# A diffusion block on one Trainium2 core: the queries' inverse norm moved into the attention's exponential, and the context's row pieces spaced ten weights apart

## The chip, the cores and the metric

The kernel runs on one NeuronCore of one Trainium2 chip. The metric is the device time of one launch in microseconds (us). Three runs of the kernel before took 1333.79, 1327.81 and 1338.1 us; their median is 1333.79. A fourth execution was profiled. It took 1332.48 us, and its profile spans 1330.7 us from the first to the last instruction, so 1.8 us lie outside the span.

## The reference, cut to what matters

One layer over 512 latent tokens with 256 context tokens beside them. Both are normalised and modulated, then projected; the context gives only keys and values. Queries and keys get an RMS norm per head (128 channels), the latents' also a rotation; the softmax runs over 768 keys.

```python
q = _rope(_rmsnorm(_heads(p, OFF_Q, N_Q_HEADS), q_norm_g[l]), cos, sin) * q_scale
k = _rope(_rmsnorm(_heads(p, OFF_K, N_KV_HEADS), k_norm_g[l]), cos, sin)
kc = _rmsnorm(_heads(pc_kv, 0, N_KV_HEADS), k_norm_g[l])       # context
s = jnp.einsum('bqhgd,bkhd->bhgqk', qi, k, preferred_element_type=jnp.float32)
w = jax.nn.softmax(s, axis=-1).astype(v.dtype)
```

The inverse norm is one positive number per token and head. A product of a query row with it multiplies that row's 768 scores by the same number, so it may be applied to the query or to the scores.

## The kernel before, in words

**Products in three matmuls.** Every fp32 operand is split into a high part and a low rest. ScalarE (ACT) writes the high part (line 163), VectorE (DVE) subtracts it from the source and writes the rest (line 164), and each product is then three matmuls (lines 305 to 307): high with high, with the low part of the weights (306), and low data with high weights. A weight piece is 128x1024. Three of every five go to `whi` and `wlo`; the other two go as two halves of 128x512 to tiles called `s`.

**The weights' queue.** `stream` lists every piece in order of use. `start_load` issues its DMA (line 202, or 205 for the first piece of a chain) on the SP queue as soon as one of some six raw buffers is free; `get` splits the pieces ahead of the one that the matmuls take (`split_piece`). Some pieces are sums: a chain tile `R` (four of them, one per piece `pc` 0 to 3) gets `R += wr` on DVE (line 250), or an accumulating DMA from GpSimd's queue (line 261), which is issued once the split that reads `R` is done. For the product P7 DVE forms `wr = R - wr` (line 252), which needs both the load of `wr` and the accumulating DMA into `R`.

**The groups.** The input projection runs in eight groups, `KINDS = (qz, qz, qz, gate, gate, kv, gate, gate)`. Each has seven products of four weight pieces, in the order P1, Q5, P2, Q6, P7, Q3, Q4: a scheme with seven half-size products in the place of eight. A piece keeps TensorE busy for about 2.7 us (12 matmuls). A `qz` group gives 512 channels of queries and 512 of a gate; when a half of the queries is ready, `qz_done` calls `rotated`.

**`rotated`** (lines 838 to 858) takes 256 tokens by 4 heads. ACT squares and sums per token and head into `ss`, 8 columns of `sums`; DVE multiplies by the cosines (849) and the sines (851); GpSimd turns the sums into inverse roots (`root_of`); DVE adds the two products (854), multiplies the sum by the inverse norm (855, a 128x1024 product), and transposes 32x32 blocks (857). The result goes to DRAM (`q_d`). `kv_done` calls the same function for the keys.

**The context's rows.** The context's normalised and modulated rows are made in four parts, while the two gate groups 3 and 4 run. `context_piece` says after which weight piece each is made: counted from group 3's first piece, after the pieces 18, 24, 30 and 36 of the two groups' 56. `context_row(i, raw)` makes one: four DVE multiplications (line 976), one subtraction (979), six more with shifts (985), ACT's additions of the shifts (988, 989), then a store of 896 KB to DRAM (990, `cf_d`). All four use the one tile `qr`, so a part's first multiplication waits until the part before has been stored. Its 512 KB of raw rows take one of the weights' raw buffers. `context_norm` and `context_spread`, which make the factor of the tokens, run from a list of jobs, one job per piece. The kv group (5) reads `cf_d` back, and puts its rotation tables into `qr` (lines 821 and 822).

**Attention.** For each of 12 heads and 4 blocks of 128 queries, `scores(i)` makes 128x768 scores in PSUM; DVE takes the negated row maximum (line 1130), ACT the exponential with this as bias and its row sum (1132). `turn(i)` transposes the probabilities on TensorE (1148) and splits them, `divide(i)` puts the inverse sum into the gate's rows (1141, 1142), `values` multiplies with the values. Branch B's products (`fill`) lie between.

**What sets the order.** The code above fixes what depends on what. The framework's scheduler then lists each engine's instructions by its own estimates of durations, and each engine runs its list in order. So an edit can move instructions that it does not name.

Of the kernel before, what the change touches and what calls it, by code (L numbers as in the profile page):

```python
# [12 lines left out]
ACT = mybir.ActivationFunctionType  # L13
ALU = mybir.AluOpType
# [4 lines left out]
P = 128  # L19
# [4 lines left out]
HD = 128  # L24
# [3 lines left out]
NKEY = T + C  # L28
# [36 lines left out]
def context_piece(g, name, pc):  # L65

    n = 28 * (g - NQZ) + 4 * ONE_GROUP.index(name) + pc
    if n % 2 == 0 and 0 <= n < 8:
        return "cn", n // 2
    if n % 6 == 0 and 18 <= n < 42:  # L70
        return "cr", n // 6 - 3

# [33 lines left out]
def block_kernel(ctx, tc, xT, ctx_rows, ctx_toks, x, c_row, w_ss, w_gate, vecs, qkg, rope, dft_c, dft_s,  # L108
                 w_start, w_g, w_pab, w_o, final_g, out):
    nc = tc.nc  # L110
# [28 lines left out]
    def uid(s):  # L139
        cnt[0] += 1  # L140
        return f"{s}{cnt[0]}"
# [148 lines left out]
    def slot_tile(p, shape, dt):  # L290
        return p[0].tile([P] + list(shape), dt, tag=p[1], bufs=1, name=uid("s"))

    def take(shape, dt=F32, pool=None):
        p = next((p for p in free if p[0] is pool), free[0])
        free.remove(p)
        t = slot_tile(p, shape, dt)
        home[id(t)] = p, t
        return t

    def give(*ts):  # L300
        free.extend(home.pop(id(t))[0] for t in ts)

    def mm3(o, ah, al, bh, bl, start, stop, cont=False):

        nc.tensor.matmul(o, ah, bh, start=start, stop=False, skip_group_check=cont)  # L305
        nc.tensor.matmul(o, ah, bl, start=False, stop=False, skip_group_check=cont)  # L306
        nc.tensor.matmul(o, al, bh, start=False, stop=stop, skip_group_check=cont)  # L307
# [11 lines left out]
    small = const.tile([P, 6 * KK], F32, name="small")  # L319
# [57 lines left out]
    for g in range(LAST + 1):  # L377
        for name in ONE_GROUP:
            if (g, name) == (LAST, "Q4"):
                stream_keys(0)  # L380
            if g == KV:
                f = CTX_FORMS.index(next(f for n, f, _, _ in PRODUCTS if n == name))
                stream(("cf", name), cf_d[:, :, f].rearrange("i p j c -> p i j c"), 1024, 8, dst=ctx_tiles)
            stream_product(name, g, w_g[g], BY_DVE_GATES)
            for pc in range(4):
                p = context_piece(g, name, pc)
                if p:
                    src, cols = (ctx_toks[p[1]], 1024) if p[0] == "cn" else (ctx_rows[p[1]], 4 * C)
                    stream(p, src, cols, 1, "raw")
                    todo.insert(len(todo) - 4 + pc, todo.pop())  # L390
# [12 lines left out]
    for name in OUT_GROUP:  # L403
        stream_product(name, 8, w_o[1], BY_DVE_OUT)
        if name in DONE:
            half, c = DONE[name]
# [292 lines left out]
    def pair(tag, skip=0):  # L699
        if tag == "y":  # L700
            last_y[0] += 1 + skip
            return psp.tile([P, 2, 512], F32, tag=f"y{last_y[0] % 2}", bufs=1, name=uid(tag))
        return psp.tile([P, 2, 512], F32, tag=tag, bufs=2, name=uid(tag))
# [21 lines left out]
    class Group:  # L725
# [12 lines left out]
        def run(self, name):  # L738
# [10 lines left out]
            for pc in range(4):  # L749
                w = get((name, self.g, pc))  # L750
                for k in range(2):
                    for t in range(2):
                        self.mm(a, form, 2 * pc + k, t, w, start and pc == 0 and k == 0,
                                pc == 3 and k == 1, cont=not start)
                if self.more:
                    self.more.products(name, which, pc, w, start)
                for f, h, ready in between(self.g, name, pc):
                    if ready:
                        self.forms[f][4 * h : 4 * h + 4] = split_form(whole[f, h])
                    else:  # L760
                        make_form(f, h)
                job()
                p = None if self.last else context_piece(self.g, name, pc)
                if p:
                    (context_squares if p[0] == "cn" else context_row)(p[1], get(p))
# [65 lines left out]
    sums, stats = small[:, :32], gain.rearrange("p k j -> p (k j)")  # L831

    def root_of(ss, n=HD):

        nc.gpsimd.tensor_scalar(ss, ss, 1.0 / n, EPS, op0=ALU.mult, op1=ALU.add)
        nc.gpsimd.tensor_tensor(ss, ss, mhalf[:, : ss.shape[-1]], op=ALU.pow)

    def rotated(half, v, t2):

        v = v.rearrange("p t (h d) -> p t h d", h=4)  # L840
        r, t2 = new_q(), t2.rearrange("p t (h d) -> p t h d", h=4)
        ss = sums[:, 8 * half : 8 * half + 8]
        r5 = lambda w: w.rearrange("p h (a f j) -> p h a f j", a=2, f=2)
        for b in range(2):
            cosb, sinb = (turning[:, i, 2 * half + b, None, :].broadcast_to([P, 4, HD]) for i in range(2))
            for h in range(4):
                nc.scalar.activation(t2[:, b, h, :], v[:, b, h, :], ACT.Square,
                                     accum_out=ss[:, 4 * b + h : 4 * b + h + 1])
            nc.vector.tensor_tensor(r[:, b], v[:, b], cosb, op=ALU.mult)
            for f in range(2):  # L850
                nc.vector.tensor_tensor(r5(t2[:, b])[:, :, :, f, :], r5(v[:, b])[:, :, :, 1 - f, :],
                                        r5(sinb)[:, :, :, f, :], op=ALU.mult)
        root_of(ss)
        nc.vector.tensor_tensor(t2, r, t2, op=ALU.add)
        nc.vector.tensor_tensor(t2, t2, ss.rearrange("p (t h) -> p t h", t=2)[:, :, :, None].broadcast_to([P, 2, 4, HD]),
                                op=ALU.mult)
        nc.vector.transpose(r.rearrange("p t h d -> p (t h d)"), t2.rearrange("p t h d -> p (t h d)"))
        return r

    def qz_done(half, c, v, t):  # L860

        if c:
            e = pair("x" if half else "y")
            nc.scalar.activation(e, v, ACT.Tanh, scale=0.5)
            nc.vector.scalar_tensor_tensor(v, e, 1.0, v, op0=ALU.add, op1=ALU.mult)
            r = v.rearrange("p t (h d) -> p t h d", h=4)
        else:
            r = rotated(half, v, pair("y"))
        for b in range(2):
            t = 2 * half + b  # L870
            if c:
                nc.scalar.dma_start(z_d[4 * group.g : 4 * group.g + 4, :, t, :].rearrange("h p d -> p h d"), r[:, b])
            else:
                nc.scalar.dma_start(q_d[group.g, t].rearrange("p (h d) -> p h d", h=4), r[:, b])
# [3 lines left out]
    def kv_done(half, c, v, t):  # L878


        r = v.rearrange("p t (g d) -> p t g d", g=4) if c else rotated(half, v, pair("y", 1) if half else pair("x"))
        for b in range(2):
            if c:
                nc.scalar.dma_start(by_group(v_d[:, :, 2 * half + b, :]), r[:, b])
            else:
                nc.scalar.dma_start(k_d[2 * half + b].rearrange("p (h d) -> p h d", h=4), r[:, b])
# [147 lines left out]
    for g, kind in enumerate(KINDS):  # L1034
# [6 lines left out]
        elif g == KV + 1:  # L1041
            qzs.close()
            gvs, gvp = region("gvp", "right", reuse_waits="tile")
            hl_pools += range(MORE_HL)
        group = Group(g, forms, new_ev, {"qz": qz_done, "kv": kv_done, "gate": gate_done}[kind], {"a": "x", "b": "y", "c": "x"})
        if g == KV:
            group.more = Context()
# [70 lines left out]
    probs, pts, branch = {}, {}, {}  # L1118
    NSTEP = 4 * NH

    def scores(i):
        h, t = divmod(i, 4)
        kh, kl = kv[h // GQ][:2]
        s = slice(t * P, (t + 1) * P)
        qh, ql = qs[h][:, 0, s], qs[h][:, 1, s]
        sc = flat(pair("x"))
        for a, b in ((0, 512), (512, 768)):
            mm3(sc[:, a:b], qh, ql, kh[:, a:b], kl[:, a:b], True, True)
        mx = stats[:, 4 * (i % 4) : 4 * (i % 4) + 4]
        nc.vector.tensor_reduce(mx[:, 0:1], sc[:, :NKEY], axis=AX.X, op=ALU.max, negate=True)  # L1130
        probs[i] = take((NKEY,))
        nc.scalar.activation(probs[i], sc[:, :NKEY], ACT.Exp, bias=mx[:, 0:1], accum_out=mx[:, 1:2])  # L1132
        if t == 3:
            give(qs.pop(h))

# [56 lines left out]
    for i in range(NSTEP + 3):  # L1192
        h, t = divmod(i, 4)
        if i < NSTEP:
            if t == 1 and h + 2 < NH:
                load_head(h + 2)
            if i == 24:
                load_row(0)
            elif i == 28:
                silu_of_row(0)  # L1200
            if i % 12 == 10 and i // 12 + 1 < NKV:
                get_keys(i // 12 + 1)
            scores(i)
# [80 lines left out]
    for n, j in enumerate(CHUNKS):  # L1284
# [9 lines left out]
        for pc, t in products(j, accs) if n else first:  # L1294
# [4 lines left out]
            if pc > 3:  # L1299
                y = ybs[j, pc - 4]  # L1300
# [277 lines left out]
```

## Time and profile before

| what | value |
|---|---|
| runs of the kernel before | 1333.79, 1327.81, 1338.1 us |
| profiled execution: time, span | 1332.48 us, 1330.7 us |
| TensorE (PE) matmuls | 1293.6 us, 97% of the span, 6522 instructions |
| weight loads into TensorE (PEld) | 1055.5 us, 79% |
| VectorE (DVE) | 987.1 us, 74% |
| ScalarE (ACT) | 654.4 us, 49% |
| GpSimd (POOL) | 136.5 us, 10% |
| mean granted TensorE clock | 0.994 of full speed |
| DMA | 291.28 MB, mean 219 GB/s |

The page gives busy time by engine. As the matmuls are pipelined and overlap, 97% says that TensorE hardly ever stands still; the views that matter are the waits (who waited for whom, in total, how often, the longest) and the timeline of a stretch, where a row is an instruction with its start, its length, and in brackets the idle time of its engine before it and what ended that. Names of tiles stand as `out<-in`, without their numbers.

### The profile page before, as it was taken

The page shows a single profiled execution, that of the slowest core. Times are in us where ns is not written, and L with a number is a line of the kernel's source. Part 1 is how long each engine was busy: PE and PEld are TensorE (multiplying, and loading weights), DVE is VectorE, ACT ScalarE, POOL GpSimd, SP SyncE. Part 2 cuts the span into 40 slices and gives each one's busy share as a digit, 9 for nine tenths or more (in the row PEclk, how much of TensorE's full clock was granted, in tenths as well). Part 3 has the DMA queues.
Part 4 walks back from the last instruction along what each step waited for, and adds up shares of the span by engine and source line. Part 5 has one row for each costly group of instructions (what it writes and reads, how often), then busy time and mean ns, then how long its engine had stood idle before and what let it go on. Part 6 is the DMA issues. An engine that isn't in the chain of part 4 may idle for free. (4 is left out here: it accounts for less than half of the span.)

```text
span 1330.7 us, 17467 instructions
## 1 busy us (share of the span) xinstructions
PE 1293.6 (97%) x6522; PEld 1055.5 (79%) x6522; DVE 987.1 (74%) x1299; ACT 654.4 (49%) x1018; POOL 136.5 (10%) x186
## 2 busy tenths in 40 slices
PE   7999999999999999999998999999999999999996
PEld 3566887888888887888887888888888888878884
DVE  4655889888778878648485667778676789787677
ACT  5322655555555454444253555667565233464534
POOL 1110011110211111011021020000000100110210
PEclk9999999999999999999998999999999999999999
DMA  9996677877888899877659798442113988778973
GB/s 383 398 380 251 221 193 201 217 216 228 196 301 212 278 279 247 274 165 180 202 145 279 236 202 235 119 95 69 44 48 119 342 337 310 190 157 242 229 209 127
DMA packets 125718, 291.28 MB, mean 219 GB/s; under 512 B 46784, under 2 KB 60608, under 8 KB 121280
## 3 DMA queue, kind: packets, MB, share of 16 engines
q1 hardware_dynamic: 88912, 176.10, 40.0%
q0 software_dynamic: 21168, 91.24, 28.4%
q10 hardware_dynamic: 15552, 22.81, 4.9%
q8 instruction: 51, 0.84, 0.3%
q14 instruction: 35, 0.29, 0.1%
HBM read 263.37 MB, written 26.75 MB: 218 GB/s over the span
## 5 line engine op out<-in xcount | busy, mean ns | idle before, releaser
L163 ACT ACTIVATE whi<-wr 128x1024 fp32r<-128x1024 f32 (+1 forms) x129 | 135.4, 1052 | 188.5 <-PE y L307 77.4
L306 PE MATMUL y<-wlo,s 128*128 128x512 f32 x544 | 213.7, 393 | 5.3 <-DVE wlo L164 5.3
L306 PE MATMUL x<-wlo,s 128*128 128x512 f32 x548 | 214.4, 391 | 3.6 <-DVE wlo L164 3.6
L305 PE MATMUL y<-whi,s 128*128 128x512 f32 x544 | 214.9, 395 | 1.1 <-ACT s L772 1.1
L305 PE MATMUL x<-whi,s 128*128 128x512 f32 x548 | 214.5, 391 | 0.7 <-ACT whi L163 0.4
L307 PE MATMUL x<-whi,s 128*128 128x512 f32 x548 | 213.9, 390 | 0.0
L307 PE MATMUL y<-whi,s 128*128 128x512 f32 x544 | 213.3, 392 | 0.0
L164 DVE TENSOR_TENSOR wlo<-wr,whi 128x1024 fp32r<-128x1024 f32 (+1 forms) x129 | 155.4, 1210 | 54.1 <-ACT whi L163 53.6
L163 ACT ACTIVATE whi<-R 128x1024 fp32r<-128x1024 f32 x115 | 121.3, 1059 | 130.3 <-PE y L307 58.5
L164 DVE TENSOR_TENSOR wlo<-R,whi 128x1024 fp32r<-128x1024 f32 x115 | 139.7, 1219 | 50.3 <-ACT whi L163 50.1
L306 PEld LDWEIGHTS x<-wlo,s 128*128 128x128 f32 x548 | 103.3, 188 | 25.6 <-DVE wlo L164 4.5
L306 PEld LDWEIGHTS y<-wlo,s 128*128 128x128 f32 x544 | 102.8, 189 | 25.3 <-DVE wlo L164 6.2
L305 PEld LDWEIGHTS y<-whi,s 128*128 128x128 f32 x544 | 102.6, 189 | 23.6 <-ACT s L772 1.5
L305 PEld LDWEIGHTS x<-whi,s 128*128 128x128 f32 x548 | 103.3, 188 | 22.7 <-ACT whi L163 0.8
L307 PEld LDWEIGHTS x<-whi,s 128*128 128x128 f32 x548 | 103.3, 188 | 21.7
L307 PEld LDWEIGHTS y<-whi,s 128*128 128x128 f32 x544 | 102.7, 189 | 21.6
L306 PE MATMUL x<-s,s 128*128 128x512 f32 (+1 forms) x284 | 106.7, 376 | 0.0
L307 PE MATMUL x<-s,s 128*128 128x512 f32 (+1 forms) x284 | 105.7, 372 | 0.0
L305 PE MATMUL x<-s,s 128*128 128x512 f32 (+1 forms) x274 | 103.9, 379 | 1.0 <-ACT s L1132 0.9
L261 POOL DMA_DIRECT2D R<-in_w_g x64 | 55.1, 866 | 440.5 <-DVE wlo L164 314.9
L163 ACT ACTIVATE s<-wr 128x512 fp32r<-128x512 f32 (+2 forms) x98 | 65.2, 681 | 64.7 <-PE y L307 25.9
L164 DVE TENSOR_TENSOR s<-wr,s 128x512 fp32r<-128x512 f32 (+2 forms) x98 | 71.4, 750 | 27.6 <-ACT s L163 26.7
(273 smaller groups left out, 2240.7 us busy)
## 6 DMA issues: line engine op xcount, KB each, us to landing
wr<-in_w_g SPq DMA_DIRECT2D x128, 512.0 KB, 4.7
R<-in_w_g POOLq DMA_DIRECT2D x64, 512.0 KB, 7.0
wa<-in_w_ss POOLq DMA_DIRECT2D x28, 1024.0 KB, 8.7
R<-in_w_g SPq DMA_DIRECT2D x32, 512.0 KB, 5.0
wr<-in_w_pab SPq DMA_DIRECT2D x32, 512.0 KB, 5.0
wr<-in_w_gate SPq DMA_DIRECT2D x32, 512.0 KB, 5.5
wr<-in_w_o SPq DMA_DIRECT2D x24, 512.0 KB, 5.3
R<-in_w_o POOLq DMA_DIRECT2D x24, 512.0 KB, 7.1
```

The source lines that it names most:

```text
L163: nc.scalar.activation(hi, src, ACT.Copy)
L164: return nc.vector.tensor_tensor(lo, src, hi.bitcast(F32), op=ALU.subtract)
L261: nc.gpsimd.dma_start(chain[e.pc], e.nxt, accum_op=ALU.add)
L305: nc.tensor.matmul(o, ah, bh, start=start, stop=False, skip_group_check=cont)
L306: nc.tensor.matmul(o, ah, bl, start=False, stop=False, skip_group_check=cont)
L307: nc.tensor.matmul(o, al, bh, start=False, stop=stop, skip_group_check=cont)
```

## The change

Two edits.

1. `context_piece` puts the context's four row parts at the pieces 14, 24, 34 and 44, ten apart, in the place of 18, 24, 30 and 36.
2. The queries are no longer multiplied by their inverse norm in `rotated`. The inverse norms stay in SBUF, 16 columns for each of the three qz groups (`qss`, in columns of `small` that nothing reads any more at that time), so the queries' sums no longer share the columns of `sums`. In `scores` a DVE product of 128x1 multiplies the negated maximum by them, and the exponential takes them as its factor (`scale=r`). The keys are treated as before.

```diff
-    if n % 6 == 0 and 18 <= n < 42:
-        return "cr", n // 6 - 3
+    if n % 10 == 4 and 14 <= n < 54:
+        return "cr", n // 10 - 1
...
+    qss = [small[:, 32:48], small[:, 48:64], small[:, 80:96]]
+
+    def rotated(half, v, t2, ss, scaled):
...
-        ss = sums[:, 8 * half : 8 * half + 8]
...
         root_of(ss)
         nc.vector.tensor_tensor(t2, r, t2, op=ALU.add)
-        nc.vector.tensor_tensor(t2, t2, ss.rearrange("p (t h) -> p t h", t=2)[:, :, :, None].broadcast_to([P, 2, 4, HD]),
-                                op=ALU.mult)
+        if scaled:
+            nc.vector.tensor_tensor(t2, t2, ss.rearrange("p (t h) -> p t h", t=2)[:, :, :, None].broadcast_to([P, 2, 4, HD]),
+                                    op=ALU.mult)
...
-            r = rotated(half, v, pair("y"))
+            r = rotated(half, v, pair("y"), qss[group.g][:, 8 * half : 8 * half + 8], False)
...
         mx = stats[:, 4 * (i % 4) : 4 * (i % 4) + 4]
+        r = qss[h // 4][:, 4 * t + h % 4 : 4 * t + h % 4 + 1]
         nc.vector.tensor_reduce(mx[:, 0:1], sc[:, :NKEY], axis=AX.X, op=ALU.max, negate=True)
+        nc.vector.tensor_tensor(mx[:, 0:1], mx[:, 0:1], r, op=ALU.mult)
         probs[i] = take((NKEY,))
-        nc.scalar.activation(probs[i], sc[:, :NKEY], ACT.Exp, bias=mx[:, 0:1], accum_out=mx[:, 1:2])
+        nc.scalar.activation(probs[i], sc[:, :NKEY], ACT.Exp, bias=mx[:, 0:1], scale=r, accum_out=mx[:, 1:2])
```

The scheduler's lists move with it, in three places that matter below. In the lists the line numbers of the changed kernel are larger by 3 to 5 from `rotated` on.

**VectorE in group 0, where the first half of the queries is rotated.** `y` is the rotated half, `ev` and `S` are other forms and results of the group. Before:

```order
L854 TENSOR_TENSOR y_1836<-qr,y_1836 128x1024
L686 TENSOR_TENSOR ev_1940<-s_926,S_68 128x512
L855 TENSOR_TENSOR y_1836<-y_1836,small 128x1024
L687 TENSOR_TENSOR ev_1940<-ev_1940,s_927 128x512
L857 STREAM_TRANSPOSE qr<-y_1836 128x1024
```

Now:

```order
L855 TENSOR_TENSOR y_1836<-qr,y_1836 128x1024
L686 TENSOR_TENSOR ev_1939<-s_926,S_68 128x512
L859 STREAM_TRANSPOSE qr<-y_1836 128x1024
L687 TENSOR_TENSOR ev_1939<-ev_1939,s_927 128x512
L686 TENSOR_TENSOR ev_1939<-s_1094,S_68 128x512
```

The 128x1024 product by `small` is gone, and all behind it moves up by one place.

**VectorE in group 4, from the end of Q5's splits over P2's.** `s_347<-R_1236` is the last half of Q5's last piece; `s_451` and `s_585` are P2's first piece, the next three `wlo` its others; `L976` (now `L979`) is the context's fourth part; `L252` forms a piece of P7. `DMASW1` is the accumulating DMA into `R_1236`, `DMASW6` that into `R_1233`. Before:

```order
L164 TENSOR_TENSOR s_347<-R_1236,s_346 128x2x256 [waits Activation_49]
L976 SCALAR_TENSOR_TENSOR qr<-wr_3994,gain,qr 128x2x128 [waits DMAHW6_49,DMAHW4_49]
L164 TENSOR_TENSOR s_451<-wr_3950,s_450 128x2x256 [waits PE_49,Activation_49]
L164 TENSOR_TENSOR s_585<-wr_3950,s_584 128x2x256 [waits PE_49,Activation_49]
L976 SCALAR_TENSOR_TENSOR qr<-wr_3994,gain,qr 128x2x128 x2
L164 TENSOR_TENSOR wlo_4050<-wr_4033,whi_4049 128x1024 [waits DMAHW7_49,Activation_49]
```

Now:

```order
L252 TENSOR_TENSOR wr_4097<-R_1233,wr_4097 128x1024 [waits DMAHW3_49,DMASW6_49]
L164 TENSOR_TENSOR s_347<-R_1236,s_346 128x2x256 [waits Activation_49]
L986 TENSOR_TENSOR small<-shift 128x1
L986 TENSOR_TENSOR small<-shift 128x1 [waits DVE_49]
L164 TENSOR_TENSOR s_451<-wr_3950,s_450 128x2x256 [waits PE_49,Activation_49]
L164 TENSOR_TENSOR s_585<-wr_3950,s_584 128x2x256 [waits PE_49,Activation_49]
L252 TENSOR_TENSOR wr_4174<-R_1236,wr_4174 128x1024 [waits DMAHW1_49,DMASW1_49]
L164 TENSOR_TENSOR wlo_4024<-wr_4003,whi_4023 128x1024 [waits DMAHW6_49,Activation_49]
L164 TENSOR_TENSOR wlo_4042<-wr_4021,whi_4041 128x1024 [waits DMAHW7_49,Activation_49]
L164 TENSOR_TENSOR wlo_4064<-wr_4039,whi_4063 128x1024 [waits DMAHW0_49,DVE_49,Activation_49]
L164 TENSOR_TENSOR s_228<-R_1233,s_227 128x2x256 [waits DVE_49,Activation_49]
L979 SCALAR_TENSOR_TENSOR qr<-wr_4115,gain,qr 128x2x128 [waits DMAHW6_49,DMAHW4_49]
```

The fourth part has gone behind all of P2's splits, and two of P7's four differences have come ahead of P2's second piece; before, all four of them stood behind the context's part.

**VectorE in the attention, between two maxima.** Before:

```order
L1130 TENSOR_REDUCE gain<-x_6806 128x1
L164 TENSOR_TENSOR s_6616<-s_6693,s_6615 128x512
L164 TENSOR_TENSOR ptl_6734<-tp_6795,pth_6733 128x6x128
L1130 TENSOR_REDUCE gain<-x_6847 128x1
L1141 RECIPROCAL gain<-gain 128x1
```

Now:

```order
L1134 TENSOR_REDUCE gain<-x_6811 128x1
L164 TENSOR_TENSOR s_6617<-s_6696,s_6616 128x512
L164 TENSOR_TENSOR ptl_6738<-tp_6800,pth_6737 128x6x128
L1135 TENSOR_TENSOR gain<-gain,small 128x1
L1134 TENSOR_REDUCE gain<-x_6853 128x1
```

The maximum's 128x1 product does not stand directly behind its maximum here; two splits lie between them.

More of the change, by code (lines that the diff above doesn't have):

```diff
@@ L836, in root_of @@
         nc.gpsimd.tensor_tensor(ss, ss, mhalf[:, : ss.shape[-1]], op=ALU.pow)
-    def rotated(half, v, t2):
+    qss = [small[:, 32:48], small[:, 48:64], small[:, 80:96]]
+    def rotated(half, v, t2, ss, scaled):
         v = v.rearrange("p t (h d) -> p t h d", h=4)
         r, t2 = new_q(), t2.rearrange("p t (h d) -> p t h d", h=4)
-        ss = sums[:, 8 * half : 8 * half + 8]
         r5 = lambda w: w.rearrange("p h (a f j) -> p h a f j", a=2, f=2)
@@ L878, in kv_done @@
     def kv_done(half, c, v, t):
-        r = v.rearrange("p t (g d) -> p t g d", g=4) if c else rotated(half, v, pair("y", 1) if half else pair("x"))
+        r = v.rearrange("p t (g d) -> p t g d", g=4) if c else rotated(
+            half, v, pair("y", 1) if half else pair("x"), sums[:, 8 * half : 8 * half + 8], True)
         for b in range(2):
```

## The prediction

> **What bounds the kernel now.** I read the page's busy times first, then the waits of TensorE, then the stretches around its longest waits in the timeline.
>
> ```profile
> PE 1293.6 (97%) x6522; PEld 1055.5 (79%) x6522; DVE 987.1 (74%) x1299; ACT 654.4 (49%) x1018; POOL 136.5 (10%) x186
> ```
>
> TensorE is busy for 97% of the span, and the change leaves its matmuls as they are. So the time can fall only by what TensorE waits, and can rise only by new waits. The view of who waited for whom, for TensorE (us in total, times, longest):
>
> ```profile
> PE pd L459 <- DVE s L458: 8.7, 1, 8.7
> PE y L306 <- DVE wlo L164: 5.3, 2, 4.5
> PE x L306 <- DVE wlo L164: 3.6, 2, 2.5
> ...
> PE y L307 <- DVE s L164: 1.2, 1, 1.2
> ...
> PE x L305 <- ACT s L1132: 0.9, 3, 0.3
> ```
>
> The first is the start and stays. Of the others the change can reach three: the 2.5 (in group 4, at 512 us, among the context's rows), the 1.2 (in group 0, at 229 us, where queries are rotated), and the 0.9 of the attention's exponential. The 4.5 lies at 719 us, where neither the program nor VectorE's list changes. Windows around the 2.5 (length, TensorE busy and matmuls, granted clock, DMA share, GB/s):
>
> ```profile
> 504.00:508.00 4.00, 4.00 (x19) 1.00 0.90 296
> 508.00:512.00 4.00, 1.83 (x9) 1.00 0.98 391
> 512.00:514.00 2.00, 1.70 (x4) 0.59 0.55 124
> 514.00:516.00 2.00, 2.00 (x6) 0.56 0.79 256
> 516.00:518.00 2.00, 2.00 (x10) 1.00 0.72 272
> ```
>
> The wait costs more than itself: in the 4 us behind it the clock is 0.59 and 0.56, and 10 matmuls run where 19 fit (first row). Nine missing at 4.0 / 19 = 0.21 us are 1.9 us. With a second wait of 0.2 at 518 us, the place costs 2.5 + 0.2 + 1.9 = 4.6 us. It is the largest thing that the change can win.
>
> **Part 1: the product that leaves the rotation.** VectorE's timeline in group 0:
>
> ```profile
> 217.99 1.22 DVE L855 TENSOR_TENSOR y<-y,small 128x1024 f32<-128x1024 f32 x1
> 219.12 0.68 DVE L687 TENSOR_TENSOR ev<-ev,s 128x512 f32<-128x512 f32 x1
> ...
> 227.80 1.21 DVE L164 TENSOR_TENSOR s<-S,s 128x1024 fp32r<-128x1024 f32 x1
> 228.93 1.21 DVE L164 TENSOR_TENSOR wlo<-wr,whi 128x1024 fp32r<-128x1024 f32 x1
> ```
>
> The product occupies VectorE for 219.12 - 217.99 = 1.13 us. Six of the eight such products leave (two halves in three groups): 6.8 us of VectorE. Five are hidden: no wait of TensorE in the list follows them. The first is not: from 217.99 to 229 these rows run without idle time, and the split that ends at 229.0 is what TensorE waited 1.2 for. It moves up by 1.13, so this gives **-1.1 us**. Bounds: -1.2, the whole wait; 0, if something else ends as late, such as ACT's half of the same split. I take -1.1, as VectorE's rows are seamless.
>
> **Part 2: the context's rows.** VectorE's timeline in group 4:
>
> ```profile
> 491.54 0.69 DVE L164 TENSOR_TENSOR s<-R,s 128x512 fp32r<-128x512 f32 x1
> 500.23 0.49 DVE L976 SCALAR_TENSOR_TENSOR qr<-wr,gain,qr 128x256 f32<-128x256 f32 x1 [8.00 <-DMA cf_d<-qr]
> 500.64 1.29 DVE L164 TENSOR_TENSOR s<-wr,s 128x512 fp32r<-128x512 f32 x2
> ...
> 502.63 1.22 DVE L164 TENSOR_TENSOR wlo<-wr,whi 128x1024 fp32r<-128x1024 f32 x1
> ...
> 509.89 1.23 DVE L252 TENSOR_TENSOR wr<-R,wr 128x1024 f32<-128x1024 f32 x1 [2.48 <-DMA wr<-in_w_g]
> 511.03 1.22 DVE L164 TENSOR_TENSOR wlo<-wr,whi 128x1024 fp32r<-128x1024 f32 x1
> ```
>
> The fourth part stands ahead of P2's splits in VectorE's list and waits 8.0 for the third part's store. Behind it P2's weights queue, so their raw buffers come free late, and a load that P7 needs lands only at 509.9; the split behind that is the one TensorE waits for. In the new list the fourth part stands behind P2's last split. The 8.0 go, and with them all of the **4.6**.
>
> But the same list has put two of P7's differences (line 252) ahead of P2's second piece, and the second waits for the accumulating DMA into the fourth chain tile. That DMA can only be issued when Q5's last half has been split, which itself now stands behind the first difference, and that one waits for the first accumulating DMA. GpSimd's timeline, and each of these two DMAs alone in the view of DMA issues (the last column is us to landing):
>
> ```profile
> 485.41 0.85 POOL L261 DMA_DIRECT2D R<-in_w_g  x1 [45.34 <-DVE wlo L164]
> ...
> 492.53 0.85 POOL L261 DMA_DIRECT2D R<-in_w_g  x1 [0.41 <-DVE s L164]
> ```
>
> ```profile
> R<-in_w_g POOLq DMA_DIRECT2D x1, 512.0 KB, 9.6
> ```
>
> ```profile
> R<-in_w_g POOLq DMA_DIRECT2D x1, 512.0 KB, 12.4
> ```
>
> So the first lands at 485.4 + 9.6 = 495.0. Then come the difference (1.1) and the half split (0.6): 496.7, and the fourth DMA starts there and not at 492.5. Before, it landed at 492.5 + 12.4 = 504.9, in a stretch where the DMA share is 0.9 and more; as the same bytes move, I let it land at 504.9 again, 8.2 after its issue. P2's first piece is split meanwhile. Then follow the difference (1.1) and the split (1.2): 507.2. TensorE's timeline says when it takes that piece's low part:
>
> ```profile
> 504.23 0.39 PE L306 MATMUL x<-wlo,s 128*128 128x512 f32 x1
> ```
>
> So it waits 507.2 - 504.2 = 3.0, and with 1.9 at the low clock loses 4.9. The splits of the two pieces behind take 1.2 each against 2.7 of matmuls, so they are not late. Part 2 comes to -4.6 + 4.9 = **+0.3 us**: one wait in the place of another. Bounds, from all eight such DMAs in 484:524 and the four of group 3 (405:425):
>
> ```profile
> DMA to landing us min/median/max: 6.7/10.8/13.7
> ```
>
> ```profile
> DMA to landing us min/median/max: 5.5/6.3/7.3
> ```
>
> Best: issue at 492.5 and 7.3 as in group 3 give 499.8, the split is done at 502.1, TensorE does not wait: -4.6. Worst: the first takes 13.7 (499.1), the fourth starts at 500.8 and takes 10.8 (511.6), the split is done at 513.9, 9.7 late: 9.7 + 1.9 - 4.6 = +7.0. I take +0.3, as the durations of this very stretch are the nearest.
>
> The Trainium skill (TensorE: Matmul & The Clock Gate, "Why this matters for your kernels") says that gaps over some 3 us bring the half clock. By that rule the old gap of 2.5 would have cost no clock, and the new one of 3.0 might: -2.7 + 4.9 = +2.2 for this part, 1334.7 in all. The row decides against it for the old gap: 0.59 stands behind 2.5 us.
>
> What else moves: the fourth part now stands some 4.5 pieces of weights later in the list (all of P2 and half a piece), at 2.7 us each 12 us, and with it its store, the load of the kv group's tables and the reading back of `cf_d`. SP's timeline has the first readings:
>
> ```profile
> 526.69 1.51 SPq L202 DMA_DIRECT2D wr<-cf_d  x2
> ```
>
> From 504.2, where P2's second piece begins, 19 pieces of 2.7 us and the 4.6 lost lead to the kv group at about 560. Twelve us of delay and a DMA of some 11 us still fit (550), so this costs nothing; without that cover the kv group would start late by what is over. Two 128x1 differences of shifts (line 983) move into the start, 0.15 us each on an engine that idles there: nothing.
>
> **Part 3: the attention.** Each of the 48 steps gets a 128x1 product on VectorE between maximum and exponential, and the exponential a factor from SBUF. No such pair is in the trace; the nearest rows are a 128x1 product (min/median/max in ns), and ACT's 128x512 rows with such a factor and without:
>
> ```profile
> L983 DVE TENSOR_TENSOR small<-shift x8: 145/150/155, 381.2 to 491.4; 128x1 f32<-128x1 f32 x8
> ```
>
> ```profile
> L1406 ACT ACTIVATE s<-s,r 128x512 f32<-128x512 f32 x4 | 2.7, 713 | 0.2 <-DVE r L1391 0.2
> L1350 ACT ACTIVATE s<-s 128x512 f32<-128x512 f32 x4 | 2.5, 634 | 6.3 <-DVE s L1381 3.4 <-DVE s L1374 2.5 <-DVE r L1391 0.4
> ```
>
> So a step's exponential ends 0.15 + 0.08 = 0.23 us later, more where the list puts a split between maximum and product (0.6 to 0.95 us). TensorE does not follow at once: it waited for the exponential three times in 48 steps, 0.9 in all, as other matmuls lie between. Bounds: 0, and 48 x 0.23 = 11.0 if every step's delay came through. Nearest are the three steps that had no slack: 3 x 0.23 = 0.7, and a little for a step whose slack a split uses up: **+1.0 us**.
>
> **Sum.** -1.1 + 0.3 + 1.0 = +0.2. From the profiled execution's 1332.48 us that is **1332.7 us**. That execution is 1.3 below the median of the runs shown (1333.79), well within their 10 us of spread.
>
> **The rivals.**
>
> The wait goes and nothing takes its place: -1.1 - 4.6 + 1.0, or 1327.8 us. For it: the 8.0 us are certainly gone, and group 3's DMAs landed in 5.5 to 7.3. Against: the DMA share here is 0.9 to 0.98, and the new order makes the DMA start later. Chance 0.3.
>
> The accumulating DMAs are as slow as the slowest of this stretch: part 2 is +7.0, 1339.4 us. It decides once the fourth lands after 504.9. Chance 0.13.
>
> Slower by the attention: the exponential becomes what TensorE waits for in each step, 1332.7 - 1.0 + 11.0 = 1342.7 us. It sets in where a step's exponential has less than 0.23 us to spare; against it, 45 of 48 steps showed no wait. Chance 0.12.
>
> **How the numbers follow.** The forecast, one wait for another, has 0.45, with a range of its own from 1329 to 1337 (its terms by a few us). All cases lie between 1327.8 and 1342.7; with a median's own uncertainty that leaves **1325 to 1341** for eight in ten. A measurement of this kernel can tell about 1% (13 us) from no change. No case reaches 1320.5; the slowest two together would pass 1347. So faster 0.03, within 1% 0.93, slower 0.04.
>
> **What would show it.** Right: the waits of TensorE no longer have the 1.2 of group 0; no wait of VectorE for `cf_d<-qr` of 8 us in group 4; instead one of VectorE's line 252 for `R<-in_w_g`, and a wait of about 3 us of TensorE near 503, with clock near 0.5 behind it. TensorE's waits for the exponential are 1 to 2 us in total. Wrong: no wait of TensorE between 495 and 525 (then the first rival), or one of 5 us or more; waits for the exponential of 5 us or more (then the last).

## The result and the profile after

The changed kernel takes 1337.38 us (median of 22 runs, 1334.36 to 1342.37), the kernel before, on the same chips, 1333.97 (22 runs). The ratio is 1.0035, with a 95% interval from 1.0023 to 1.0046: 3.1 to 6.1 us slower, best value 4.7. I had forecast +0.2. The profiled execution of the changed kernel took 1336.57 us, its span is 1334.8, so 4.1 above that of before.

TensorE's waits after the change, from the view of who waited for whom (us in total, times, longest):

```profile
PE x L306 <- DVE wlo L164: 6.5, 2, 5.4
PE y L306 <- DVE wlo L164: 4.4, 2, 3.9
...
PE tp L1153 <- ACT s L1137: 1.4, 2, 0.9
...
PE x L305 <- ACT s L1137: 0.9, 3, 0.4
...
PE y L305 <- DVE s L1177: 0.2, 1, 0.2
```

The 1.2 of group 0 is gone, as forecast. The wait of 2.5 in group 4 is gone too, but one of 5.4 stands in its place. The waits for the exponential (lines 1137 and 1153 are the old 1132 and 1148) are 2.3 instead of 0.9. VectorE's timeline in group 4:

```profile
492.34 0.69 DVE L164 TENSOR_TENSOR s<-R,s 128x512 fp32r<-128x512 f32 x1
...
496.75 1.23 DVE L252 TENSOR_TENSOR wr<-R,wr 128x1024 f32<-128x1024 f32 x1 [3.45 <-DMA wr<-in_w_g]
497.89 0.69 DVE L164 TENSOR_TENSOR s<-R,s 128x512 fp32r<-128x512 f32 x1
...
498.63 1.29 DVE L164 TENSOR_TENSOR s<-wr,s 128x512 fp32r<-128x512 f32 x2
507.36 1.23 DVE L252 TENSOR_TENSOR wr<-R,wr 128x1024 f32<-128x1024 f32 x1 [7.44 <-DMA R<-in_w_g]
508.51 3.49 DVE L164 TENSOR_TENSOR wlo<-wr,whi 128x1024 fp32r<-128x1024 f32 x3
```

This is the chain that I had forecast, but for one link (below): two differences (line 252) ahead of P2's second piece, a half split between them (497.89), then 7.4 us in which the second one waits for the accumulating DMA, and only then the split that TensorE needs. GpSimd's timeline has that DMA's issue, right behind the end of the half split at 498.6 (the bracket names another of VectorE's rows), and the view of DMA issues, for that one, its time to landing:

```profile
498.87 0.85 POOL L261 DMA_DIRECT2D R<-in_w_g  x1 [5.15 <-DVE small L986]
```

```profile
R<-in_w_g POOLq DMA_DIRECT2D x1, 512.0 KB, 8.5
```

Issued at 498.87 and not at 496.7, landed at 507.4 and not at 504.9. The duration is as forecast (8.5 for 8.2); the issue is 2.2 late, because the first accumulating DMA was issued at 488.0 and not at 485.4 (and landed 8.2 us later, at 496.2), and the first difference waited a little longer still, for its own load (496.75). TensorE, and the stretch around its wait (length, TensorE busy and matmuls, granted clock, DMA share, GB/s):

```profile
509.78 0.79 PE L306 MATMUL x<-wlo,s 128*128 128x512 f32 x1 [5.42 <-DVE wlo L164]
```

```profile
506.00:508.00 2.00, 0.00 (x0) 1.00 0.21 64
508.00:510.00 2.00, 0.22 (x1) 0.90 0.00 0
510.00:512.00 2.00, 2.00 (x5) 0.50 0.53 127
512.00:514.00 2.00, 2.00 (x8) 0.75 0.87 305
```

Behind the wait the clock is 0.50 and 0.75. And in the last 4 us of the wait the DMA engines have hardly anything to do (0.21, then 0.00): VectorE stands still, so no raw buffer comes free, so no load is issued between 500.3 and 509.7 us. SP's queue, which issues the loads, waits for VectorE's splits (between 495 and 515 us; the 9.4 is this stop):

```profile
SPq L202 <- DVE wlo L164: 10.9, 3, 9.4
```

To see where the 4.1 us came from I numbered the 6522 matmuls in each trace and subtracted, for each number, the start in the first execution of before. This difference is flat, and jumps at a few places. Each column is what it grows by across one place, in us (group 0: 218 to 265 us; group 4: 486 to 552; the wait at 719: 705 to 735; the attention: 821 to 1024). The last column but one adds the three places that the change can reach, with the mean of the three executions in the old order (-0.5) as group 4's reference; the last is the timed ratio less one, as us of 1334, with its interval.

```
execution          group 0  group 4   719   attention |  sum  timed (interval)
before               0        0       0       0
before, again        0.0     -1.5    -1.1    +0.1
changed             -1.2     +2.6    -1.3    +2.9     |  +4.2*  +4.7 (+3.1 to +6.1)
changed, again      -1.2     +1.5    -0.3    +2.7
rows_only            0.0     +1.9    +0.1    +0.1     |  +2.4   +3.3 (+1.5 to +5.3)
norm_only           -1.2      0.0    -0.8    +2.9     |  +1.7*  +1.3 (-0.3 to +3.1)
no_factor           -1.2     +1.1    -0.7    +0.1     |  +0.5   +1.5 (-0.4 to +3.3)
product_only        -1.2     +2.2    -0.6    +2.6     |  +4.1   +5.3 (+2.8 to +7.9)
factor_only         -1.2     +1.4    -0.6    +0.5     |  +1.2   +2.5 (+0.4 to +4.8)
late_differences    -1.2     -3.0    -0.2    +2.9     |  -0.8   -0.1 (-2.1 to +1.7)
first_late          -1.2     +1.7    -0.8    +2.8     |  +3.8   +5.5 (+3.3 to +7.6)
second_late         -1.1     -4.9    -0.4    +3.1     |  -2.4   -0.3 (-2.1 to +1.6)
rows_late            0.0     -4.3    +0.6    +0.1     |  -3.7   -3.1 (-5.5 to -0.7)
min_late            -1.1     -2.2     0.0    +0.9     |  -2.0*  -2.3 (-4.4 to  0.0)
* changed: mean of its two executions in group 4 and the attention; norm_only: in the old order, group 4 set to nothing;
  min_late: without the 2.1 us of a wait of its own at 428 us (below); with them the sum is +0.1
```

The start (before 218 us) and the end (behind 1266 us) differ by up to 3.9 and 1.9 us from the first execution of before, in the same kernel too (before, again: 3.1 at the start), and are left out. In the first execution of the changed kernel they are +1.2 and -0.1, and with the four columns they make the 4.1. The sum lies in the timed interval in ten of the eleven rows; second_late misses it by 0.3.

### The profile page after: what moved, and what is told of

The parts are those of the page before. It is cut to its first block, busy times and chain, and to the rows that moved or that the text cites. A ratio compares the mean times of both kernels' runs of the same rounds, so it can differ in the third digit from the quotient of the medians.

```text
span 1334.8 us, 17511 instructions
## 1 busy us (share of the span) xinstructions
PE 1295.9 (97%) x6522; PEld 1056.8 (79%) x6522; DVE 983.4 (74%) x1341; ACT 656.5 (49%) x1018; POOL 135.2 (10%) x186
## 5 line engine op out<-in xcount | busy, mean ns | idle before, releaser
L252 DVE TENSOR_TENSOR wr<-R,wr 128x1024 f32<-128x1024 f32 x40 | 48.8, 1223 | 52.5 <-DMA wr<-in_w_g 27.8
```

The lines of the kernel that those rows point to most:

```text
L252: nc.vector.tensor_tensor(src, chain[e.pc], src, op=ALU.subtract)
```

## The experiments

Theory: the result is a sum of separate places, -1.2 in group 0 (the product that left), some +2 in group 4 (the second difference's wait), +2.9 in the attention (maximum, product, factor). Rivals: chance in the DMAs, one part shifting the other, and for the attention the factor instead of the product.

**Each half of the change alone.** rows_only is the kernel before with the new spacing:

```
-    if n % 6 == 0 and 18 <= n < 42:
-        return "cr", n // 6 - 3
+    if n % 10 == 4 and 14 <= n < 54:
+        return "cr", n // 10 - 1
```

> Only the spacing of the context's rows is changed; the queries' norm stays a product in the rotations. Theory (three local effects that add): the wait of about 1.2 us in group 0 stays, the waits for the exponential stay at 0.9 us, and the stretch 500 to 530 us shows the changed kernel's wait of about 5.4 us with the lower clock behind it, so the loss of that stretch is about 7.0 us instead of 4.7: +2.3 there, and between 0 and -1.3 at 719 us, so +1 to +2.3 in all against the kernel before (1333.5 to 1334.8 by its profiled 1332.48). Rival (the longer wait comes from the shortened rotation list or from chance in the DMAs, not from the spacing): the wait near 503 to 510 is 3 us or less, and the time is that of before or 1 to 2 us below it.

norm_only is the changed kernel with these lines put back.

> Only the norm is moved into the exponential; the context's rows stay six pieces apart. Theory: -1.2 us in group 0, the wait of 2.5 us at 512 us as before, and +3.0 us in the attention (835 to 1010 us): +1.8 in all, 1334.3 by the profiled execution of before; +0.5 if the gain of 1.3 at 719 us belongs to this part. Rival (the attention's rise belongs to chance, or to what the spacing shifted): attention as before, within 0.5 us, and 1.2 us faster in all, 1331.3.

The waits of rows_only (TensorE, the whole span) and VectorE's second difference:

```profile
PE x L306 <- DVE wlo L164: 4.8, 2, 3.7
...
PE y L307 <- DVE s L164: 1.2, 1, 1.2
...
PE x L305 <- ACT s L1132: 0.9, 3, 0.3
```

```profile
505.85 1.23 DVE L252 TENSOR_TENSOR wr<-R,wr 128x1024 f32<-128x1024 f32 x1 [7.65 <-DMA R<-in_w_g]
```

The wait of group 4 came with the spacing alone (3.7, not 5.4), with the same wait of VectorE in front of it; group 0 and the attention stayed as before. In norm_only group 4 stayed as before and both other places moved. The halves add (timed +3.3 and +1.3, together +4.6 against the change's +4.7), and neither shifts the other. The sizes in group 4 vary: the expected 5.4 was too exact.

**Where the wait of group 4 comes from.** late_differences is the changed kernel with

```
-            nc.vector.tensor_tensor(src, chain[e.pc], src, op=ALU.subtract)
+            with tc.issue_after(last_split[0].ins) if e.key[1] == 4 else nullcontext():
+                nc.vector.tensor_tensor(src, chain[e.pc], src, op=ALU.subtract)
```

so that each of group 4's four differences stands behind the split of the piece before it. In first_late the condition has `and e.pc == 0` as well (the first difference alone is moved), in second_late `and e.pc == 3` (the second alone). The rest of VectorE's list moves by a few rows around it; in first_late the second difference itself comes to stand one piece sooner, ahead of P2's first piece.

> The changed kernel, but in group 4 each of P7's differences (line 252) is queued behind the split of the piece of weights before it, so none stands ahead of P2's pieces. Theory (the wait of 5.4 us is that of the second difference for the fourth accumulating DMA, standing in front of P2's second piece): no wait of TensorE over 0.5 us between 495 and 530 us, clock 1.0 there, 7 us less than the changed kernel: 1329.6 by its profiled 1336.57. Rival (loads of this stretch are late whatever stands in VectorE's list: the wait moves to P2's or P7's own pieces): a wait of 2 us or more of TensorE between 500 and 545 us, and a gain of less than 4 us.

> The changed kernel, but of group 4's differences only the first one (for chain tile R_1233) is queued behind the split of the piece before it; the second one (R_1236) stays ahead of P2's second piece. Theory (the second difference's wait for the fourth accumulating DMA is the stall): VectorE's wait for R<-in_w_g of 5 us or more stays, and with it a wait of TensorE of 2 us or more near 505 to 512 us; if the DMA takes 8.6 us from its issue as before, issued at about 495 us, the wait of TensorE is about 2 us, if it lands at 510 us as in late_differences, 7 us. Rival (the first difference, which holds up the fourth DMA's issue, is the cause): no wait of TensorE over 1 us between 495 and 530 us.

> The changed kernel, but of group 4's differences only the second one (R_1236) is queued behind the split of the piece before it; the first one stays ahead. Theory: no wait of TensorE over 1.2 us between 495 and 530 us, and 5 to 6 us below the changed kernel in that stretch. Rival (the first difference is the cause): the wait of 3.7 us or more stays.

The stretch 500 to 530 us of late_differences and of second_late (columns as above; 134 matmuls in 30 us are the full rate):

```profile
500.00:530.00 30.00, 29.35 (x130) 1.00 0.77 230
```

```profile
500.00:530.00 30.00, 30.00 (x134) 1.00 0.87 250
```

first_late: VectorE's difference with the split behind it (P2's first piece, the two halves in `s`), TensorE's wait, the DMA that the difference waits for as GpSimd issued it, and that DMA alone in the view of DMA issues:

```profile
504.16 1.23 DVE L252 TENSOR_TENSOR wr<-R,wr 128x1024 f32<-128x1024 f32 x1 [13.27 <-DMA R<-in_w_g]
505.31 1.28 DVE L164 TENSOR_TENSOR s<-wr,s 128x512 fp32r<-128x512 f32 x2
```

```profile
PE x L306 <- DVE s L164: 5.0, 1, 5.0
```

```profile
491.12 0.85 POOL L261 DMA_DIRECT2D R<-in_w_g  x1 [0.54 <-DVE small L986]
```

```profile
R<-in_w_g POOLq DMA_DIRECT2D x1, 512.0 KB, 13.0
```

The second difference is the cause: with it behind the splits nothing is lost in this stretch (second_late), with both behind, 1.2 us of waits are left (late_differences), and with the first alone moved the wait is 5.0 us again. late_differences was expected 7 us below the changed kernel with no wait over 0.5; it is 5.0 below by the table and 4.8 by the timed ratios, and its longest wait is 0.6.

first_late also shows that the late issue accounts for a part of the late landing only. The DMA was issued at 491.1, 7.7 us sooner than in the changed kernel, and landed at 504.1, 3.2 us sooner: it took 13.0 instead of 8.5. TensorE waited about as long all the same, because the difference stands one piece sooner here: TensorE waits for `s` and not for `wlo`, some 2.7 us sooner in its work. My expectation of some 2 us had the landing nearly right (495 + 8.6 = 503.6), but it left out this move in the list.

**What of the attention costs.** All three variants leave the queries' norm out of the result. no_factor has neither product nor factor:

```
-        nc.vector.tensor_tensor(mx[:, 0:1], mx[:, 0:1], r, op=ALU.mult)
...
-        nc.scalar.activation(probs[i], sc[:, :NKEY], ACT.Exp, bias=mx[:, 0:1], scale=r, accum_out=mx[:, 1:2])
+        nc.scalar.activation(probs[i], sc[:, :NKEY], ACT.Exp, bias=mx[:, 0:1], accum_out=mx[:, 1:2])
```

product_only keeps the product's line, with `ones[:, 0:1]` for `r`, and drops the factor; factor_only drops the product's line and keeps `scale=`, with `ones[:, 0:1]` for `r`.

> The changed kernel without the factor in the exponential and without the 128x1 product; the queries' norm is left out altogether, the attention's steps are those of the kernel before. Theory (product and factor make each step's exponential end later, and that costs 3.0 us): the drift of TensorE's matmuls against the kernel before does not grow by more than 0.5 us between 835 and 1010 us, and the time is 3.0 us below the changed kernel's: 1333.6 by its profiled 1336.57. Rival (the attention's rise comes from where the work before it ends, so another phase against the DMAs and the splits): the rise of 2 to 3 us stays, 1336 to 1337.

> The changed kernel with the 128x1 product (by a column of ones) but without the factor in the exponential; the queries' norm is left out. Theory (the product is the cost: in 21 of 48 steps a split of 0.5 to 2.0 us stands between maximum and product in VectorE's list, and the exponential waits for the product): the drift against the kernel before grows by 2.0 to 2.9 us between 835 and 1010 us. Rival (the factor's 0.09 us in every exponential is the cost): it grows by 0.7 us or less.

> The changed kernel with a factor in the exponential (a column of ones) but without the 128x1 product; the queries' norm is left out. Theory (the product is the cost): the exponential takes 0.99 us instead of 0.90, and the drift against the kernel before grows by 0.9 us or less between 835 and 1010 us. Rival (the factor is the cost): it grows by 2 us or more.

ScalarE's waits for the maximum or its product between 835 and 1012 us, of before, the changed kernel, product_only and factor_only:

```profile
ACT s L1132 <- DVE gain L1130: 10.7, 13, 1.4
```

```profile
ACT s L1137 <- DVE gain L1135: 17.2, 20, 1.6
```

```profile
ACT s L1137 <- DVE gain L1135: 17.0, 20, 1.7
```

```profile
ACT s L1137 <- DVE gain L1134: 7.8, 11, 1.4
```

With the product ScalarE waits 17 us in 20 steps, without it 8 to 11 us in 11 to 13. The table says the same of TensorE: +2.6 with the product alone, +0.5 with the factor alone, +0.1 with neither. So it is not the phase in which the attention starts: no_factor has the same work ahead of it, and late_differences and second_late, with -3.0 and -4.9 in group 4, grow by 2.9 and 3.1. The factor's price per step is what was forecast (groups by line, the exponential in the changed kernel and in product_only, mean ns: 991 and 901):

```profile
L1137 ACT ACTIVATE s<-x,gain,small 128x768 f32<-128x768 f32 x45 | 44.6, 991 | 18.3 <-DVE gain L1135 17.2 <-DVE gain L1146 1.2
```

```profile
L1137 ACT ACTIVATE s<-x,gain 128x768 f32<-128x768 f32 x45 | 40.5, 901 | 18.9 <-DVE gain L1135 17.0 <-DVE gain L1146 1.9
```

**Without a separate product, and a better version.** min_late is late_differences with maximum and product in one instruction:

```
-        nc.vector.tensor_reduce(mx[:, 0:1], sc[:, :NKEY], axis=AX.X, op=ALU.max, negate=True)
-        nc.vector.tensor_tensor(mx[:, 0:1], mx[:, 0:1], r, op=ALU.mult)
+        nc.vector.tensor_scalar(probs[i], sc[:, :NKEY], nr, None, op0=ALU.mult, op1=ALU.min, accum_out=mx[:, 0:1])
```

(`nr` is the negative factor's column, made by GpSimd; `probs[i]` is taken ahead of it.) rows_late is rows_only with the edit of late_differences.

> late_differences, but the maximum and its product are one instruction: sc times the negative factor, with the minimum accumulated (its 128x768 output goes to the tile that the exponential then overwrites); GpSimd makes the negative factors. Theory (the product behind the maximum is the cost of the attention): the attention's growth falls from 2.9 to 0.9 us or less, so 2 us below late_differences: -1.2 -3.0 +0.9 against before, 1329.2 by the profiled 1332.48. Rival (any instruction that makes the exponential end later costs the same, and the accumulating one takes over 1.1 us): the growth stays at 2 us or more.

> The kernel before with the new spacing of the rows, and with group 4's differences (line 252) queued behind the split of the piece before them; the norm stays in the rotations. Theory (effects add): against before nothing in group 0 and in the attention, and -3.0 us in 500 to 560 us, as in late_differences: 1329.5 by the profiled 1332.48, a ratio of 0.998. Rival (the gain of late_differences in group 4 needs the shorter rotations): the wait there is 2 us or more again and the time that of before.

The new instruction in min_late, with the reading of its accumulator:

```profile
L1135 DVE TENSOR_SCALAR_CACHE_REDUCE s<-x,nq 128x768 f32<-128x768 f32 x47 | 47.6, 1012 | 3.2 <-PE y L1168 1.4 <-PE x L307 1.4
...
L1135 DVE DVE_READ_ACCUMULATOR s<-x,nq 128x1 f32 x46 | 3.8, 83 | 0.0
```

It takes 0.14 us more than the maximum's 0.95, nearly as much as the product (0.16), but nothing stands between its halves, and the attention grows by 0.9 instead of 2.9. So it is not the product's own time that costs most. In VectorE's trace rows of 0.67 us or more stand between maximum and product in 22 of the changed kernel's 48 steps, in 20 of them splits. From the start of a step's maximum to the end of its exponential (each pair subtracted, mean of 48) it takes:

```
                         us      over before   attention's growth
before, no_factor       2.23
factor_only             2.33        0.10          0.5
min_late                2.38        0.15          0.9
product_only            2.69        0.46          2.6
changed                 2.78        0.55          2.9
```

The growth is some 5 to 6 times the mean delay, as if 5 or 6 of the 48 steps let it through to TensorE. That is an average: in the changed kernel the delay comes through at some ten places, by 0.1 to 0.8 us, and 0.8 is won back at 934 us, where a wait of before (0.28) is gone. Of the 0.55, 0.09 is the factor and 0.19 the product with its start (from the maximum's end, in the 26 steps with nothing long between them); the other 0.27, by subtraction, is what stands in front of the product.

rows_late came out as expected in its time: 1329.43 us against 1332.76 for before beside it, ratio 0.9977 (0.9959 to 0.9995); group 4 gave -4.3, though, and not -3.0. min_late is 1330.09, 0.9983 (0.9967 to 1.0000), 2.2 us below late_differences by the ratios. In its trace TensorE also waits 1.8 at 428 us, behind a store of queries (8.2 us of VectorE waiting for `q_d<-qr`). No other run has this wait of TensorE, though product_only's VectorE waits 8.3 us for the same store, so it stays unexplained.

So moving the norm gains next to nothing in this kernel: -1.2 and +2.9 as the change does it, -1.1 and +0.9 at best (min_late). What gains is group 4, and rows_late, which leaves the norm where it was, has that alone.

**Chance.** Each kernel was profiled once more.

> The changed kernel once more. Theory (the wait of 5.4 us in group 4 and the gain of 1.3 us at 719 us contain some us of chance, the rises of group 0 and the attention none): a wait between 3.7 and 5.5 us in group 4; the place at 719 us within 1 us of before's; -1.2 in group 0 and +2.9 in the attention to 0.1 us. Rival (each place repeats): 5.4 us in group 4 and -1.3 at 719 us again.

> The kernel before once more. Theory: the wait of 2.5 us at 512 us again (2.4 in norm_only), the wait at 719 us between 3.9 and 4.8 us with one or two low-clock stretches, nothing else between 60 and 1290 us that moves by over 0.3 us against the first execution. Rival (these waits are chance as a whole): a wait at 512 us under 1 us or over 4.

TensorE's waits between 495 and 545 us in the second execution of before, and its stretch 500 to 530:

```profile
PE y L306 <- DVE s L164: 1.8, 1, 1.8
PE x L306 <- DVE wlo L164: 1.0, 1, 1.0
```

```profile
500.00:530.00 30.00, 27.25 (x119) 1.00 0.93 252
```

Two waits of 1.0 and 1.8 instead of one of 2.5, and the clock stayed at 1.00, so the place cost 1.5 us less than in the execution on which I had built the term. The expected 2.5 did not repeat. At 719 us the same kernel gained 1.1 from one execution to the other; the 1.3 of the changed kernel there is of that size, and group 0 and the attention repeat to 0.2 (0.1 was expected). In its second execution the changed kernel waited 3.8 in group 4.

## Why the prediction was right and wrong

**Part 1 was right.** -1.1 forecast, -1.10 to -1.17 measured in all ten executions without the product in the rotations, 0.0 in the others.

**Part 2 had the mechanism, and both of its sizes were off.** The new wait stands where it was put, behind the instruction that was named, for the DMA that was named. The term read "-4.6 + 4.9". That the whole of the old place could go is so: second_late, which loses nothing there, is 4.9 below before. But the size came from one execution; the next showed 1.5 less, a third (norm_only) the same 4.6, so 4.1 on average. The 4.9 came from a wait of 3.0 with 1.9 of low clock behind it; the six executions in the new order waited 3.7 to 5.4 and lost 4.6 + 1.1 to 4.6 + 2.6, on average 6.4. So the part is +2.3 and not +0.3: it lies inside the stated bounds (-4.6 to +7.0). In the profiled execution the wait of 5.4 is over the 5 us that I had named as a sign of being wrong. Of the steps, "the fourth DMA starts there" (496.7) was nearly right in rows_only (497.15) and 2.2 early in the changed kernel, where the first accumulating DMA landed at 496.2 and not at 495.0, and the first difference's own load still later; "I let it land at 504.9 again" was 1.0 early in rows_only (505.85) and 2.5 in the changed kernel (507.36); that a later issue makes the DMA shorter held (first_late). The 1.9 of low clock fits a clock of 0.50 that lasts 3.4 us (half of that, 1.7, is lost); in three of the six executions it lasted 6.8 (last section). The other value that I worked out for this part, +2.2, left the old wait without its low clock, while two of three executions in the old order show it; that +2.2 is near the measured +2.3 is luck. Its time adds up to 1334.6 and not 1334.7.

**Part 3 failed by its size.** The step was "Nearest are the three steps that had no slack: 3 x 0.23 = 0.7, and a little for a step whose slack a split uses up". The three steps were too few (5 to 6 on average), and the 0.23 left out what the list puts in front of the product, though the text had named it: the mean delay is 0.55. The measured term is +2.9. min_late, which has nothing in between, grows by 0.9, near the forecast's +1.0, but as some 6 times 0.15 and not 3 times 0.23.

**The sum** is -1.2 + 2.3 + 2.9 = +4.0, against 4.7 timed. It was also wrong that runs of this kernel can tell only some 13 us from no change: with 22 runs the interval is 1.5 us to either side. Of the rivals, the wait that goes without replacement did not happen; the sign of the slowest accumulating DMAs came true (the fourth landed after 504.9), but by a late issue and not by a slow DMA (8.5 us), and of its +7.0 a third came; the exposed exponential set in for 5 or 6 of the 48 steps on average, not for all. The waits for the exponential that I would have read as right (1 to 2 us in total) were 2.3 (2.5 with the one for line 1177), 1.6 more than before: they understate the place by 1.3. Of this, 0.25 are waits under 0.15 us, which the view leaves out (0.34 in the changed kernel, 0.09 in before). The rest fits the way in which the view counts: from the end of the matmul before, 0.39 us after its start, while matmuls follow each other every 0.23. So it counts some 0.16 too little at each stop, and 11 stops in the place of 4 make an estimated 1.1.

**What stays open**: why the loads of group 4 come 1 to 2 us later in some executions than in others, and what makes the low clock last 3.4 us in some of them and 6.8 in others. No run has the separate product directly behind its maximum, so the share of what stands between them (0.27) is a subtraction only.

## What to carry to other kernels

A tiny dependent instruction can cost its place in the queue more than its duration (a delay of 0.46 us against 0.19 here): ask what the list can put in front of it, and fold it into its producer if that matters. When a wait leaves an in-order queue, look for the next instruction in that queue that waits for a DMA, and hold it behind what the bottleneck engine needs; here moving one difference took the whole loss of group 4 away. A wait that is read from one execution has an error of its own (1.5 us here), so a forecast that is the difference of two such waits needs both from several.

## What the runs showed of the hardware

- Where the granted clock falls. In group 4, waits of TensorE up to 1.76 us left it at 1.00 (second execution of before, above), one of 2.4 in norm_only and those of 3.7 and more brought it to 0.94 or 0.89 over 30 us. So in group 4 the edge is between 1.8 and 2.4 us. The Trainium skill (TensorE: Matmul & The Clock Gate, "Why this matters for your kernels") has it at some 3 us; the rows decide. norm_only's waits, then its stretch, then that of the second execution of the changed kernel (wait 3.8):

```profile
PE x L306 <- DVE wlo L164: 3.5, 2, 2.4
```

```profile
500.00:530.00 30.00, 27.29 (x112) 0.94 0.90 251
```

```profile
500.00:530.00 30.00, 26.20 (x106) 0.89 0.75 186
```

- It is not one edge for the whole kernel. At the start, where TensorE often stands still, the changed kernel's clock fell behind a wait of 1.25 us (the first row), and min_late's stayed at 1.00 behind one of 2.08 (the second):

```profile
38.60:42.00 3.40, 3.40 (x11) 0.51 1.01 413
```

```profile
36.60:38.00 1.40, 1.21 (x4) 1.00 1.02 424
```

- How long the low clock lasts. Between 60 and 1290 us every low phase of these traces has a clock of 0.50 and lasts 3.4 or 6.8 us, and a longer wait does not make it longer: in group 4 it is 3.4 behind the changed kernel's 5.4 and 6.8 around the 3.8 of its second execution:

```profile
509.60:513.00 3.40, 3.22 (x8) 0.50 0.60 173
```

```profile
508.10:514.90 6.80, 4.95 (x12) 0.50 0.55 166
```

- An accumulating DMA of 512 KB that is issued sooner into a busy stretch lands sooner by less: issues at 491.1 (first_late) and 498.9 (changed kernel) landed 13.0 and 8.5 us after them, so 7.7 us at the issue were 3.2 at the landing.
- A stalled VectorE can empty the DMA engines: share 0.21 and 0.00 from 506 to 510 us in the changed kernel, and 0.87 and 0.97 again from 512 to 516, once its splits had freed buffers.
